# A decoder block on one core: attention's scores as float32r passes on padded q, values once per pair of heads, a bias copy, adaLN sums and the final norm moved

## The chip, the core and the metric

The kernel runs on one NeuronCore of a Trainium2 chip. It is one launch, and what counts is the device time of that launch in microseconds (us). The engines named below are PE (TensorE, matmuls), DVE (VectorE), ACT (ScalarE), POOL (GpSimd) and SP, whose queue issues most transfers. Each engine runs its instructions in order; a transfer is issued by the queue of an engine and then runs beside all of them. The profile is one execution recorded on the chip.

## What is computed

One block for 512 tokens of width 1024: a token mixer with 8 heads of block-sparse attention (64 wide) beside a pooling branch, then a mixture of 32 experts, then a last norm. With 512 tokens there are two blocks of 256 keys, and at most one fully past block can be selected, so the attention is causal attention with a relative bias.

```python
mod = (c_act @ w_ada[l] + b_ada[l])[:, None, :]
shift1, scale1, gate1, shift2, scale2, gate2 = jnp.split(mod, N_MOD, axis=-1)
h = rms_norm(x, norm1_g[l]) * (1 + scale1) + shift1
proj = h @ w_in[l]
q, k, v, u, z_gate = jnp.split(proj, split_pts, axis=-1)
y_attn = moba_attention(q, k, v, rel_bias) @ w_branch_attn[l]
y_pool = pool_mixer(u, pool_w[l], pool_scale[l]) @ w_branch_pool[l]
g_attn, g_pool = jnp.split(jax.nn.sigmoid(z_gate + b_gate[l]), N_BRANCHES, axis=-1)
mixed = (g_attn * y_attn + g_pool * y_pool) @ w_out[l]
x = x + gate1 * mixed
h2 = rms_norm(x, norm2_g[l]) * (1 + scale2) + shift2
x = x + gate2 * hier_moe(h2, ...)
...
return rms_norm(x, norm_f_g)
```

## The kernel before

All large products are float32. A projection is made of three float32r matmuls (`mm3`): each operand is split into a high part (ACT casts, L227) and a low part (DVE or POOL subtracts, L228), and high x high, high x low and low x high are summed in PSUM.

The program has these stages, in TensorE's order.

- Input stage, 0 to 71.6 us. x is normed and transposed, the first adaLN sums (ada_ps, L257) are made, and v, the fourth k and the first u are projected while their weights arrive. Six steps over the contraction (`first`) each bring a piece of w_ada and of w_in (wvk, L149) through SP. This stage is written out by hand: its engines run the instructions in the order of the program text. The low parts of the weights of k and u (kul) are made on POOL. The bias of the heads is made once as a row of 640 numbers per head (bias_sb); it goes to DRAM as bias_d (L376) and is then copied, 128 times per head, to bias_s in DRAM (L379, 8 x 128 x 640 numbers, 2.6 MB), from which each head reads its skewed 128 x 512 bias tile bt (L483, on SP). Both copies are issued by POOL's queue.
- Projections and attention, 71.6 to 250 us. q, k, u, the pooling branch's gates zp and its projection bp, in jobs of 12 or 24 matmuls. The attention of a pair of heads (hp = 0 to 3) runs between them. For each of four tiles i of 128 queries and each of the two heads e: scores s (L492) in fp32, on the 64 rows of that head, against the n = 128 (i + 1) keys so far; add bias and take the minimum (the q are negated) on DVE (L500); exp on ACT (L505); reciprocal and scaling on DVE (L507, L508); transposes tp in blocks of 128 (L511), copied to SBUF as pt by ACT or DVE (L514, L516); values y (L520), one fp32 matmul of 128 columns for each query tile i, key tile j and head e.
- Gates and branch projections of attention, 250 to 331 us: za and ba, eight column tiles cc each (`gated`). Beside the projections of 71.6 to 331 us run 32 steps `ada_step`: each loads 512 KB of w_ada (tile ada, two buffers, through SP) and adds it, scaled by a number of c, to gacc on DVE (L580), one in four over ACT and POOL (L577, L578). Sixteen steps make one row r of sums: gacc starts with a POOL memset (L568) and a load of b_ada (L569); at its end four small matmuls gs_ps (L586) sum it over the partitions, ACT copies the result (grow, L590), and a transfer writes it to rows_d, from where it is read back (L1020).
- Output projection, second norm, router (331 to 397 us); 16 pairs of experts (397 to 845 us), whose weights, 1 MB a load, come through SP into rings of buffers.
- Tail, 845 to 871 us: the last results are added in column ranges of 512, 256 and 256; ACT squares each token tile i in two halves (`square`, L1304), DVE forms the mean (L1307, L1329), POOL the power -0.5 (L1331), and `final` scales half a tile on ACT and half on DVE and issues the output's transfer, once for each of four token tiles.

Outside the input stage a scheduler orders the instructions of each engine, from the order of the program text, the dependences and the buffers of the pools.

## Time and profile before

| what | value |
|---|---|
| time, median of 3 runs | 874.46 us (870.32 to 875.41) |
| time of the profiled execution | 872.84 us |
| its span | 871.1 us (1.7 us lie around it) |
| PE busy | 831.2 us, 95% |
| DVE, ACT, POOL busy | 408.7, 238.9, 95.8 us |
| transfers | 265.36 MB, mean 305 GB/s |

The table is an average: in the experts' stage both TensorE and the transfers are full, in the first 331 us they are not full at the same time. So each stage is read for itself.

### The profile page before, as it was taken

Reading aid. Unit: us, or ns where it says so; the run is one execution under the profiler, and the core shown is the slowest. Engines: PE = TensorE matmul, PEld = TensorE weight load, DVE = VectorE, ACT = ScalarE, POOL = GpSimd, SP = SyncE. Lnnn points to the kernel's source line nnn. Section 1 sums busy time; section 2 is a strip of 40 time slices with the busy share of each in tenths; the row PEclk is TensorE's granted clock in tenths of the full one; section 3 lists DMA queues with packets and bytes.
Section 4 is the critical chain, followed back from the end, with each engine's and each line's share of the span. In section 5 each row is a group of like instructions: output and inputs, shape, how many; then the busy total and the mean of one; then the engine's idle time right before and its main releaser. Section 6 shows DMA issues by size and latency. Waiting matters only on the chain.

```text
span 871.1 us, 12304 instructions
## 1 busy us (share of the span) xinstructions
PE 831.2 (95%) x4890; PEld 496.4 (57%) x4890; DVE 408.7 (47%) x812; ACT 238.9 (27%) x478; POOL 95.8 (11%) x114
## 2 busy tenths in 40 slices
PE   6979999999999979999999999999999999999993
PEld 4758666676678747874445544554455445544542
DVE  4343546767537766672334333433343334333425
ACT  4222434443424324553111111111111111111204
POOL 5310003321103221141000000000000000000003
PEclk9999999999999989999999999999999999999997
DMA  9971324476357666958999999999999999999942
GB/s 294 345 290 41 103 90 122 145 243 202 94 187 246 198 258 231 374 225 350 370 420 419 420 420 419 420 419 420 420 420 420 420 419 420 420 420 419 405 137 100
DMA packets 72988, 265.36 MB, mean 305 GB/s; under 512 B 8280, under 2 KB 33708, under 8 KB 50398
## 3 DMA queue, kind: packets, MB, share of 16 engines
q1 hardware_dynamic: 71150, 261.18, 77.4%
q0 software_dynamic: 1600, 3.22, 1.0%
q8 instruction: 40, 0.66, 0.3%
q14 instruction: 22, 0.18, 0.1%
q10 hardware_dynamic: 176, 0.12, 0.0%
HBM read 262.37 MB, written 4.76 MB: 307 GB/s over the span
## 4 chain that ended last, share of the span: by engine, by line
PE 77%; DMA 10%; DVE 7%; issue 2%; ACT 1%; POOL 1%; SPq 1%; POOLq 0%; DVEq 0%; ACTq 0%
PE y_ps L1258 13%; PE g_ps L1233 13%; PE u_ps L1233 13%; PE c_ps L1271 7%; PE XT_ps L1006 6%; DMA ada<-in_w_ada_dram 5%; DVE gacc L580 3%; PE s L492 2%; DMA wvk<-in_w_in_dram 2%; PE o_ps L231 2%; PE o_ps L233 2%; PE o_ps L232 2%; DMA wq<-in_w_in_dram 1%; PE y L520 1%; PE tp L511 1%
## 5 line engine op out<-in xcount | busy, mean ns | idle before, releaser
L1233 PE MATMUL g_ps<-eg,XT 128*64 128x512 f32 x512 | 112.7, 592 | 0.1
L1233 PE MATMUL u_ps<-eu,XT 128*64 128x512 f32 x512 | 112.6, 592 | 0.0
L1258 PE MATMUL y_ps<-ed,HT 128*64 128x512 f32 x496 | 110.0, 595 | 0.0
L1242 DVE TENSOR_TENSOR H<-H,u_ps 128x512 f32<-128x512 f32 x16 | 11.0, 687 | 178.2 <-PE u_ps L1233 178.2
L1275 DVE TENSOR_TENSOR acc<-acc,c_ps 128x512 f32<-128x512 f32 (+1 forms) x132 | 78.5, 665 | 0.2 <-PE c_ps L1271 0.2
L1233 PEld LDWEIGHTS u_ps<-eu,XT 128*64 128x64 f32 x512 | 36.8, 137 | 73.1 <-issue 67.9
L1233 PEld LDWEIGHTS g_ps<-eg,XT 128*64 128x64 f32 x512 | 36.6, 137 | 73.0 <-issue 70.5
L1258 PEld LDWEIGHTS y_ps<-ed,HT 128*64 128x64 f32 x496 | 34.2, 137 | 63.6 <-issue 61.5
L1271 PE MATMUL c_ps<-Y,ohT 128*128 128x512 f32 (+1 forms) x264 | 67.9, 398 | 0.3 <-DVE Y L1353 0.2
L1006 PEld LDWEIGHTS <-h 128*128 128x128 f16 x1024 | 58.2, 113 | 6.0 <-issue 5.8
L1006 PE MATMUL XT_ps<-oh,h 128*128 128x128 f16 x1024 | 60.8, 219 | 0.7 <-DVE oh L984 0.6
L1271 PEld LDWEIGHTS c_ps<-Y,ohT 128*128 128x128 f32 x264 | 46.5, 189 | 21.7 <-issue 12.2
L580 DVE SCALAR_TENSOR_TENSOR gacc<-ada,cact,gacc 128x1024 f32<-128x1024 f32 x25 | 39.1, 1572 | 20.9 <-DMA ada<-in_w_ada_dram 20.2
L1000 ACT ACTIVATE XT<-XT_ps,col,a2col 128x128 f32<-128x128 f32 x64 | 29.2, 457 | 68.5 <-PE XT_ps L1006 53.1
L1265 DVE SCALAR_TENSOR_TENSOR y_ps<-y_ps,sw,g2row 128x512 f32<-128x512 f32 (+1 forms) x33 | 24.5, 743 | 49.7 <-PE y_ps L1258 49.7
L1250 ACT COPY HT<-HT_ps 128x512 f32<-128x512 f32 x16 | 9.4, 589 | 132.8 <-PE HT_ps L1248 132.8
L998 DVE TENSOR_SCALAR XT<-XT_ps,a2col,col 128x128 f32<-128x128 f32 x64 | 26.2, 410 | 41.5 <-ACT XT L1000 41.5
L1313 POOL MEMSET nf<- 1x128 f32 x1 | 0.2, 195 | 381.8 <-PE u_ps L1233 381.8
L227 ACT CAST Y<-y_ps 128x512 fp32r<-128x512 f32 x30 | 17.6, 585 | 86.5 <-DVE y_ps L1265 86.5
L1241 ACT ACTIVATE H<-g_ps 128x512 f32<-128x512 f32 x16 | 9.6, 597 | 82.0 <-PE g_ps L1233 82.0
L228 DVE TENSOR_TENSOR Y<-y_ps,Y 128x512 fp32r<-128x512 f32 x30 | 20.8, 692 | 21.1 <-ACT Y L227 21.1
L231 PE MATMUL za_ps<-hTh,za_h 128*128 128x512 f32 x64 | 25.0, 391 | 2.8 <-DVE ga L604 2.8
(291 smaller groups left out, 1374.9 us busy)
## 6 DMA issues: line engine op xcount, KB each, us to landing
eu<-in_w_expert_up_dram SPq DMA_DIRECT2D x60, 1024.0 KB, 15.8
ed<-in_w_expert_down_dram SPq DMA_DIRECT2D x60, 1024.0 KB, 19.6
eg<-in_w_expert_gate_dram SPq DMA_DIRECT2D x56, 1024.0 KB, 14.4
ada<-in_w_ada_dram SPq DMA_DIRECT2D x40, 512.0 KB, 4.7
eg<-in_w_expert_gate_dram SPq DMA_DIRECT2D x16, 512.0 KB, 8.2
ada<-in_w_ada_dram SPq DMA_DIRECT2D x4, 1024.0 KB, 9.2
zp<-in_w_in_dram SPq DMA_DIRECT2D x4, 1024.0 KB, 7.6
za<-in_w_in_dram SPq DMA_DIRECT2D x4, 1024.0 KB, 5.9
```

The costliest lines, as they stand in the source:

```text
L227: nc.scalar.copy(dst_h, src)
L228: sub.tensor_sub(dst_l, src, dst_h.bitcast(F32))
L231: nc.tensor.matmul(ps, lhsT=ah, rhs=bh, start=start, stop=False)
L580: nc.vector.scalar_tensor_tensor(g, t, cact[:, k : k + 1], g, op0=ALU.mult, op1=ALU.add)
L998: nc.vector.tensor_scalar(dst, src, a, b, op0=ALU.mult, op1=ALU.add)
L1000: nc.scalar.activation(dst, src, AF.Identity, bias=b, scale=a)
L1006: nc.tensor.matmul(ps[:, (k % 4) * P : (k % 4 + 1) * P], lhsT=ktile(h2[i][:, a], k), rhs=oh[:, i, :], start=(i == a == 0 and k == ks[0]), ...
L1233: mm = nc.tensor.matmul(ps[64 * e : 64 * e + 64, :], lhsT=XT[:, k, 64 * e : 64 * e + 64], rhs=ws[nm](k, e), start=(k == 0), stop=(k == KD ...
L1258: nc.tensor.matmul(ps[64 * e : 64 * e + 64, :], lhsT=HT[:, k, 64 * e : 64 * e + 64], rhs=rhs(k, e), start=(k == 0), stop=(k == KE - 1),)
L1265: nc.vector.scalar_tensor_tensor(ps, ps, sw, g2row[:, cs], op0=ALU.mult, op1=ALU.mult)
L1271: nc.tensor.matmul(ps, lhsT=ohT[:, i * P : (i + 1) * P], rhs=Y[:, a], start=(a == 0), stop=(a == 1))
L1275: nc.vector.tensor_add(accv(i)[:, cs], accv(i)[:, cs], ps)
```

## The change

Five things are changed.

1. The scores. q is kept in tiles qz, one slot per head of the pair, split into a high and a low part, 128 rows each, where the 64 rows of the other head are zero (POOL clears the two tiles once). k is split as well (kk). A score tile is then three float32r passes over 128 rows (`mm3`) in place of one fp32 matmul over 64.
2. The values. pt keeps the transposed weights of all query tiles of a head, ordered by key tile j, so that one matmul for key tile j serves all later queries: 512, 384, 256 and 128 columns. They stand after all four query tiles.
3. The order. The pairs of heads run in the order 3, 0, 1, 2, with other neighbours. The copies of the bias are written into the hand-ordered input stage.
4. The adaLN sums. Steps 16 to 19 are written into the second `pool_gated`, two instead of three steps follow each cc, and the second row's sums stand in the last cc.
5. The final norm. Squares in three column ranges, the mean of the first two for all tiles at once, the power for tiles 0 and 1 together and for 2 and 3.

```diff
+                    if n == 1:
+                        nc.gpsimd.dma_start(bias_d, bias_sb)
+                    if n + 2 == len(first):
+                        nc.gpsimd.dma_start(bias_s, bias_d.unsqueeze(1).broadcast_to([HEADS, P, 640]))
...
-    bias_d = dp.tile([HEADS, 640], F32, name="bias_d")
-    nc.gpsimd.dma_start(bias_d, bias_sb)
-
-    bias_s = dp.tile([HEADS, P, 640], F32, name="bias_s")
-    nc.gpsimd.dma_start(bias_s, bias_d.unsqueeze(1).broadcast_to([HEADS, P, 640]))
...
+    def k_tile(hp):
+        kk[hp] = at.tile([P, 2, 512], F32R, tag="kk", bufs=2, name=f"kk{hp}")
+        return kk[hp][:, 0], kk[hp][:, 1]
...
+    qz = [p.tile([P, 2, 2, 512], F32R, name=f"qz{n}") for n, p in enumerate((au, at))]
+    for z in qz:
+        for e in range(2):
+            nc.gpsimd.memset(z[64 - 64 * e : 128 - 64 * e, e].bitcast(F32), 0.0)
...
-    nc.vector.tensor_copy(kT[:, 3, :], ku_ps[0])
+    split(*k_tile(3), ku_ps[0])
...
-    for hp in range(4):
+    HPS = (3, 0, 1, 2)
+    for hp in HPS:
         job(f"q{hp}", raw["q"], hp * P, KD, hTh, hTl)
...
     def qk_proj(hp):
-        nc.scalar.mul(qT[:, hp, :], proj(f"q{hp}"), -(DH ** -0.5))
+        ps, z = proj(f"q{hp}"), q_of(hp)
+        for e in range(2):
+            rows = slice(64 * e, 64 * e + 64)
+            nc.scalar.mul(z[rows, e, 0], ps[rows], -(DH ** -0.5))
+            nc.vector.scalar_tensor_tensor(
+                z[rows, e, 1], ps[rows], -(DH ** -0.5), z[rows, e, 0].bitcast(F32), op0=ALU.mult, op1=ALU.subtract
+            )
         if hp < 3:
-            nc.vector.tensor_copy(kT[:, hp, :], proj(f"k{hp}"))
+            ps = proj(f"k{hp}")
+            split(*k_tile(hp), ps)
...
             for e in range(2):
-                nc.tensor.matmul(
-                    sps[e][:, 0:n], lhsT=qT[64 * e : 64 * e + 64, hp, i * P : (i + 1) * P],
-                    rhs=kT[64 * e : 64 * e + 64, hp, 0:n], start=True, stop=True,
-                )
-            pts = []
+                ts_ = slice(i * P, (i + 1) * P)
+                mm3(sps[e][:, 0:n], z[:, e, 0, ts_], z[:, e, 1, ts_], kh[:, 0:n], kl[:, 0:n], True, True)
...
-            for j in range(i + 1):
-                for e in range(2):
-                    nc.tensor.matmul(
-                        y_ps[64 * e : 64 * e + 64, i * P : (i + 1) * P],
-                        lhsT=vsb[:, j, (2 * hp + e) * DH : (2 * hp + e + 1) * DH],
-                        rhs=pts[e][:, j * P : (j + 1) * P], start=(j == 0), stop=(j == i),
-                    )
+        y_ps = ps1.tile([P, 512], F32, tag="y", name=f"y{hp}")
+        for j in range(NT):
+            for e in range(2):
+                nc.tensor.matmul(
+                    y_ps[64 * e : 64 * e + 64, j * P :],
+                    lhsT=vsb[:, j, (2 * hp + e) * DH : (2 * hp + e + 1) * DH],
+                    rhs=pts[e][:, 512 * j : 384 * j + 512], start=(j == 0), stop=(j == NT - 1),
+                )
         split(yAh[:, hp, :], yAl[:, hp, :], y_ps)
...
-        if n % 16 == 15:
-            ps = ps1.tile([P, 512], F32, tag="y", name=f"gs_ps{r}")
...
+        if n == 15:
+            ada_rows(0)
+
+    def ada_rows(r):
...
             gated("p", 4 * h + q, mpool[h][:, q, :], zp0 if h == q == 0 else None)
-            ada_step(8 * h + 2 * q)
-            ada_step(8 * h + 2 * q + 1)
-
+            for n in range(2 + h):
+                ada_step(8 * h + (2 + h) * q + n)
+
+    qk_proj(3)
+    pool_in(0)
+    attention(3)
     qk_proj(0)
-    pool_in(0)
+    pool_out(0)
+    qk_proj(1)
     attention(0)
-    qk_proj(1)
-    pool_out(0)
-    qk_proj(2)
-    qk_proj(3)
-    attention(1)
     pool_in(1)
...
         g = gated("a", cc, None)
+        if cc == 7:
+            ada_rows(1)
         (nc.vector if cc == 7 else nc.gpsimd).tensor_add(g, g, mpool[cc // 4][:, cc % 4, :])
...
-        for n in range(min(16 + 3 * cc, 32), min(19 + 3 * cc, 32)):
+        for n in range(min(20 + 2 * cc, 32), min(22 + 2 * cc, 32)):
             ada_step(n)
...
+    STEPS_F = (slice(0, 512), slice(512, 768), slice(768, 1024))
+
+    def square(i, n, junk):
+        cs = STEPS_F[n]
+        nc.scalar.activation(junk[:, 0 : cs.stop - cs.start], accv(i)[:, cs], AF.Square, accum_out=ssf[:, i, n : n + 1])
+
+    def mean0():
+
+        nc.vector.tensor_add(msf, ssf[:, :, 0], ssf[:, :, 1])
+        nc.vector.tensor_scalar(msf, msf, 1.0 / D, EPS, op0=ALU.mult, op1=ALU.add)
+
+    def rstd_f(*tiles):
+        ts = slice(tiles[0], tiles[-1] + 1)
+        nc.vector.scalar_tensor_tensor(msf[:, ts], ssf[:, ts, 2], 1.0 / D, msf[:, ts], op0=ALU.mult, op1=ALU.add)
+        nc.gpsimd.tensor_tensor(rsf[:, ts], msf[:, ts], neghalf.broadcast_to([P, len(tiles)]), op=ALU.pow)
...
     def final(i, p, nf):
-        ms = tiny("ms", [P, 1], F32, f"msf{p}_{i}")
-        nc.vector.scalar_tensor_tensor(ms, ssf[:, i, 1:2], 1.0 / D, msf[:, i : i + 1], op0=ALU.mult, op1=ALU.add)
-        r = tiny("rs", [P, 1], F32, f"rsf{p}_{i}")
-        nc.gpsimd.tensor_tensor(r, ms, neghalf, op=ALU.pow)
+        r = rsf[:, i : i + 1]
```

How the instructions come to stand shows at three places. First POOL in the input stage, before: kul is the low part of the weights of one step, and the copy of the bias stands between the splits of the third step and those of the fourth.

```order
L228 TENSOR_TENSOR wvl_371<-wvk_111,wvh_370 128x512
L228 TENSOR_TENSOR kul_375<-wvk_111,kuh_374 128x128 x2
L379 DMA bias_s<-bias_d 1024x1x640
L228 TENSOR_TENSOR wvl_428<-wvk_116,wvh_427 128x512
L228 TENSOR_TENSOR kul_432<-wvk_116,kuh_431 128x128 x2
L228 TENSOR_TENSOR kul_489<-wvk_122,kuh_488 128x2x128 x2
L228 TENSOR_TENSOR kul_569<-wvk_128,kuh_568 128x2x128 x2
```

POOL at the same place after the change.

```order
L228 TENSOR_TENSOR kul_377<-wvk_111,kuh_376 128x128 x2
L364 DMA bias_d<-bias_sb 8x640
L228 TENSOR_TENSOR wvl_431<-wvk_116,wvh_430 128x512
L228 TENSOR_TENSOR kul_435<-wvk_116,kuh_434 128x128 x2
L228 TENSOR_TENSOR kul_492<-wvk_122,kuh_491 128x2x128 x2
L228 TENSOR_TENSOR kul_572<-wvk_128,kuh_571 128x2x128 x2
L366 DMA bias_s<-bias_d 1024x1x640
L379 MEMSET ones 128x128
L422 MEMSET qz_705 64x1024 x2
```

The copy bias_s has moved behind the last kul, and the clearing of qz stands behind it.

Second, DVE at the first softmax step of the attention (L500: scores and the bias tile bt give sm and its minimum mn), before. q_l and k_l are low parts of weights of q and k.

```order
L228 TENSOR_TENSOR k_l<-wk_656,k_h 128x512
L476 COPY kT<-k_ps 128x512
L228 TENSOR_TENSOR q_l<-wq_650,q_h 128x512
L228 TENSOR_TENSOR q_l<-wq_652,q_h 128x512
L500 ISA sm_0_0_814,mn_0_0_815<-s_0_0_810,bt_0_805 128x128
L500 ISA mn_0_0_815 128x1
L500 ISA sm_0_1_826,mn_0_1_827<-s_0_1_811,bt_1_807 128x128
```

DVE at the same place after the change.

```order
L494 SCALAR_TENSOR_TENSOR qz_705<-q_ps,qz_705 64x512 x2
L228 TENSOR_TENSOR q_l<-wq_650,q_h 128x512
L228 TENSOR_TENSOR q_l<-wq_652,q_h 128x512
L522 ISA sm_0_0_796,mn_0_0_797<-s_0_0_788,bt_0_782 128x128
L522 ISA mn_0_0_797 128x1
L494 SCALAR_TENSOR_TENSOR qz_706<-q_ps,qz_706 64x512
L522 ISA sm_0_1_807,mn_0_1_808<-s_0_1_789,bt_1_784 128x128
L522 ISA mn_0_1_808 128x1
L529 RECIPROCAL rl_0_0_801<-l_0_0_799 128x1
L530 TENSOR_SCALAR sm_0_0_796<-sm_0_0_796,rl_0_0_801 128x128
L494 SCALAR_TENSOR_TENSOR qz_706<-q_ps,qz_706 64x512
```

The step that reads bt now stands ahead of the two low parts of the second q (qz_706), and less projection work lies before it: q of pairs 3 and 0, where q and k of pair 0, q of pair 1 and a part of its k lay.

Third, POOL between the two rows of adaLN sums, before. ga are the gated branch tiles, col is what is read back from rows_d.

```order
L578 TENSOR_TENSOR gacc_1631<-gacc_1631,ada_15_2183 128x1024
L1020 DMA col_2915<-rows_d_725 128x4 x2
L723 TENSOR_TENSOR ga_2223<-ga_2223,mpool_1610 128x512
L568 MEMSET gacc_2278 128x2048
L569 DMA gacc_2278<-in_b_ada_dram 1x16x128
L723 TENSOR_TENSOR ga_2290<-ga_2290,mpool_1610 128x512
```

POOL there after the change.

```order
L603 TENSOR_TENSOR gacc_1649<-gacc_1649,ada_15_2149 128x1024
L593 MEMSET gacc_2161 128x2048
L594 DMA gacc_2161<-in_b_ada_dram 1x16x128
L754 TENSOR_TENSOR ga_2255<-ga_2255,mpool_1628 128x512
L1051 DMA col_2931<-rows_d_731 128x4 x2
L754 TENSOR_TENSOR ga_2316<-ga_2316,mpool_1628 128x512
```

The memset and the load of the second row's gacc now stand ahead of the first ga and of the reads of rows_d.

## Rows read from the trace of the kernel before

**Rows 1.** Windows by stage: length, busy us (and instructions) by engine, PE clock, transfers.

```profile
core 0: us, PE busy (x) PEld busy (x) DVE busy (x) ACT busy (x) POOL busy (x), PEclk, DMA share, GB/s
0.00:71.60 71.60, 55.65 (x406) 41.75 (x407) 29.28 (x70) 24.70 (x52) 22.67 (x40) 0.98 0.90 295
71.60:250.00 178.40, 177.06 (x842) 123.74 (x840) 104.81 (x232) 68.98 (x154) 24.74 (x25) 1.00 0.38 124
250.00:331.00 81.00, 74.85 (x312) 56.42 (x312) 53.05 (x60) 26.36 (x49) 21.99 (x15) 0.96 0.68 235
```

**Rows 2.** Waits of PE: what for, us in total, times, longest.

```profile
PE v_ps L231 <- ACT hTh L227: 5.9, 3, 3.3
PE gs_ps L586 <- issue: 3.1, 1, 3.1
PE za_ps L231 <- DVE ga L604: 2.8, 1, 2.8
PE ada_ps L257 <- DMA ada<-in_w_ada_dram: 1.8, 1, 1.8
```

**Rows 3.** Windows, columns as in the first group: behind the wait at gs_ps.

```profile
322.20:330.00 7.80, 7.80 (x20) 3.28 (x21) 3.51 (x5) 1.51 (x3) 0.00 (x0) 0.60 0.57 228
```

**Rows 4.** Transfers, 20 to 62 us: queue, packets, MB, share of 16 engines.

```profile
q0 software_dynamic: 1072, 2.65, 16.1%
```

**Rows 5.** Chain of waits, 26 to 49 us: start, us, what.

```profile
26.46 14.50 DMA wvk<-in_w_in_dram
...
42.41 2.21 POOL kul L228 x2
44.62 3.34 SPq L149
...
48.65 12.99 DMA wq<-in_w_in_dram
```

**Rows 6.** Windows in the input stage.

```profile
42.00:48.00 6.00, 2.72 (x8) 1.89 (x7) 4.44 (x8) 1.87 (x5) 2.20 (x2) 0.77 0.53 211
```

**Rows 7.** Timeline of POOL, 40 to 72 us: start, us, instruction, idle time before it.

```profile
57.70 2.23 POOL L228 TENSOR_TENSOR kul<-wvk,kuh 128x256 fp32r<-128x256 f32 x2 [13.10 <-ACT kuh L227]
```

**Rows 8.** Transfers of tile bias_s: the copy is the longest, the others are bt.

```profile
DMA to landing us min/median/max: 2.6/4.6/22.4
```

**Rows 9.** Chain of waits, 88 to 96 us.

```profile
88.80 0.42 PE s L492 x4
89.22 0.43 PE k_ps L231
...
89.88 0.24 PE k_ps L233
...
93.98 0.63 PE s L492 x4
...
95.04 0.86 PE pw_ps L552 x2
```

**Rows 10.** Timeline of PE, 132 to 140 us.

```profile
132.81 0.91 PE L492 MATMUL s<-kT,qT 64*128 64x384 f32 x2
133.65 0.50 PE L231 MATMUL u_ps<-hTh,u_h 128*128 128x512 f32 x1
...
138.85 1.12 PE L492 MATMUL s<-kT,qT 64*128 64x512 f32 x2
139.90 0.50 PE L232 MATMUL u_ps<-hTl,u_h 128*128 128x512 f32 x1
```

**Rows 11.** PE's groups by shape, 71.6 to 331 us: busy us, mean ns, idle before.

```profile
L520 PE MATMUL y<-pt,vsb 128*64 128x128 f32 x160 | 16.9, 285 | 0.0
```

**Rows 12.** The page's groups: busy us, mean ns, idle time before and its cause.

```profile
L1265 DVE SCALAR_TENSOR_TENSOR y_ps<-y_ps,sw,g2row 128x512 f32<-128x512 f32 (+1 forms) x33 | 24.5, 743 | 49.7 <-PE y_ps L1258 49.7
```

**Rows 13.** Chain of waits, 261 to 267 us.

```profile
261.95 1.82 POOL gacc L568
...
264.06 2.46 DMA gacc<-in_b_ada_dram
```

**Rows 14.** Windows in the tail.

```profile
861.00:867.00 6.00, 0.00 (x0) 0.00 (x0) 2.11 (x5) 1.88 (x3) 1.09 (x2) 0.50 0.91 354
```

More of the change, by code (lines that the diff above doesn't have):

```diff
@@ L299, in step_ku @@
             mm3(ku_ps[n], kuh[:, m, n, :], kul[:, m, n, :], hTh[:, k, :], hTl[:, k, :], k == 0, k == KD - 1)
+    bias_d = dp.tile([HEADS, 640], F32, name="bias_d")
+    bias_s = dp.tile([HEADS, P, 640], F32, name="bias_s")
     with tc.manual_schedule(engines={getattr(mybir.EngineType, n) for n in ("PE", "Activation", "DVE", "Pool")}):
@@ L405, in block_kernel @@
     vsb = at.tile([P, NT, AW], F32, name="vsb")
-    qT = at.tile([P, 4, 512], F32, name="qT")
-    kT = at.tile([P, 4, 512], F32, name="kT")
+    kk = {}
+    def k_tile(hp):
+        kk[hp] = at.tile([P, 2, 512], F32R, tag="kk", bufs=2, name=f"kk{hp}")
+        return kk[hp][:, 0], kk[hp][:, 1]
     yPh = at.tile([P, 4, 512], F32R, name="yPh")
     yPl = at.tile([P, 4, 512], F32R, name="yPl")
-    ct1 = at.tile([P, C_W - C_KEEP], F32, name="ct1")
-    pw = at.tile([P, 4, P], F32, name="pw")
+    au, au_end = pool("au", side="right", bufs=1)
+    qz = [p.tile([P, 2, 2, 512], F32R, name=f"qz{n}") for n, p in enumerate((au, at))]
+    for z in qz:
+        for e in range(2):
+            nc.gpsimd.memset(z[64 - 64 * e : 128 - 64 * e, e].bitcast(F32), 0.0)
+    ct1 = au.tile([P, C_W - C_KEEP], F32, name="ct1")
+    pw = au.tile([P, 4, P], F32, name="pw")
     nc.sync.dma_start(ct1, consts[:, C_KEEP:])
@@ L416, in block_kernel @@
     nc.gpsimd.tensor_copy(ident16, ident)
-    au, au_end = pool("au", side="right", bufs=1)
     def utile(name):
@@ L486, in attention @@
             bts.append(bt)
-        y_ps = ps1.tile([P, 512], F32, tag="y", name=f"y{hp}")
+        z, (kh, kl) = q_of(hp), (kk[hp][:, 0], kk[hp][:, 1])
+        pts = [at.tile([P, 13 * P], F32, tag=f"pt{e}", name=f"pt{hp}_{e}") for e in range(2)]
         for i in range(NT):
@@ L580, in ada_step @@
             nc.vector.scalar_tensor_tensor(g, t, cact[:, k : k + 1], g, op0=ALU.mult, op1=ALU.add)
-        if n % 16 == 15:
-            ps = ps1.tile([P, 512], F32, tag="y", name=f"gs_ps{r}")
-            for v in range(2):
-                for h in range(2):
-                    j = 32 * (2 * v + h)
-                    nc.tensor.matmul(
-                        ps[j : j + 32, :], lhsT=onesf, rhs=gacc[r][:, v, 512 * h : 512 * h + 512], start=True, stop=True
-                    )
-            t = mo.tile([P, D], F32, tag="ad", bufs=2, name=f"grow{r}")[:, 0:512]
-            nc.scalar.copy(t, ps)
-            nc.scalar.dma_start(rows_d[r].rearrange("v (h n) -> (v h) n", h=2), t[0:P:32, :])
+        if n == 15:
+            ada_rows(0)
+    def ada_rows(r):
+        ps = ps1.tile([P, 512], F32, tag="y", name=f"gs_ps{r}")
+        for v in range(2):
+            for h in range(2):
+                j = 32 * (2 * v + h)
+                nc.tensor.matmul(
+                    ps[j : j + 32, :], lhsT=onesf, rhs=gacc[r][:, v, 512 * h : 512 * h + 512], start=True, stop=True
+                )
+        t = mo.tile([P, D], F32, tag="ad", bufs=2, name=f"grow{r}")[:, 0:512]
+        nc.scalar.copy(t, ps)
+        nc.scalar.dma_start(rows_d[r].rearrange("v (h n) -> (v h) n", h=2), t[0:P:32, :])
     def gate(which, cc):
@@ L625, in block_kernel @@
     pool_out(2)
-    attention(2)
+    qk_proj(2)
+    attention(1)
     zp0 = gate("p", 0)
@@ L632, in block_kernel @@
     pool_gated(0)
-    attention(3)
+    attention(2)
     pool_gated(1)
@@ L1289, in combine_half @@
             add(i, HALF[n], back(p, n, i, ohT, Y))
-    ssf = cp.tile([P, NT, 2], F32, name="ssf")
+    ssf = cp.tile([P, NT, 3], F32, name="ssf")
     msf = cp.tile([P, NT], F32, name="msf")
+    rsf = cp.tile([P, NT], F32, name="rsf")
     os_ = {}
@@ L1385, in last_pair @@
         for i in range(NT):
-            mean0(i)
+            square(i, 1, junk[i % 2])
         c2 = backs(2)
@@ L1389, in last_pair @@
             add(i, cols_[2], c2[i])
-            if i < 3:
-                square(i, 1, junk[i % 2])
+            square(i, 2, junk[i % 2])
+        mean0()
+        rstd_f(0, 1)
         final(0, p, nf)
-        square(3, 1, junk[1])
+        rstd_f(2, 3)
         for i in range(1, NT):
@@ L1493, in block_kernel @@
         for i in range(NT):
-            for h in range(2):
-                square(i, h, ex.tile([P, 512], F32, tag="HT", name=f"junkx{i}_{h}"))
-            mean0(i)
+            for n in range(3):
+                square(i, n, ex.tile([P, 512], F32, tag="HT", name=f"junkx{i}_{n}"))
             gain(i, "x", nf)
+        mean0()
+        rstd_f(0, 1, 2, 3)
+        for i in range(NT):
             final(i, "x", nf)
```

17 lines of the change are left out of this document (8 added, 9 removed).

## The prediction

> **What bounds the kernel now.** I read the windows by stage first, then the list of TensorE's waits, then the chain of waits in the places that these two point at. The first 331 us are the only part that the change touches, apart from the last 15 us. In it TensorE is busy 55.65 of 71.6 us, then 177.06 of 178.4, then 74.85 of 81 [rows 1]. So three different limits hold. In the first stage TensorE waits for data: 5.9 us of v_ps waits are among its losses [rows 2]. In the second (projections with attention between them) it is full, so only fewer or cheaper matmuls shorten it. In the third (gates, branch projections, adaLN sums) it waits 2.8 us at za_ps and 3.1 us at gs_ps [rows 2], and behind them it runs 7.8 us at a granted clock of 0.60, between its levels of 1.2 and 2.4 GHz [rows 3]; at the full level that work needs 0.60 x 7.8 = 4.7 us, so 3.1 more are lost there.
>
> **Bias copy (first stage).** The 2.6 MB copy bias_s goes out before the splits of step 3 and runs beside the loads of the stage. Its queue q0 took 16.1% of all engines' time from 20 to 62 us, that is 0.161 x 42 = 6.8 us [rows 4]. The chain shows who pays: a wvk load of 14.50 us, then kul on POOL for 2.21, then SP, which holds the next loads 3.34 us for that kul, then the wq load of 12.99 [rows 5]. From 42 to 48 us TensorE is busy 2.72 of 6 us, while the transfers fill only 0.53 of the engines [rows 6]: the half that works is not the half that the loads in front need. The change issues the copy after the last kul, so all of this goes. Bounds: at least the 3.34 us for which SP stood, since the wvk ahead of it comes that much sooner; at most the 5.9 us of waits, 1.8 on an ada load and 6 x (1 - 0.77) = 1.4 us of low clock [rows 2, 6], 9.1 in all. The loads themselves then come late next, so I take **-6 us** (-3.3 to -9.1). A rule bears on the 0.53: the Trainium skill, "DMA: Bandwidth & Descriptors", section "Rules for kernel authors", says that an outermost dimension under 16 keeps a DMA to at most that many engines; the copy's outermost is the 8 heads, hence half of 16, and the trace agrees. By that rule the copy is as slow after the move as before.
>
> What the move costs: the bt loads need the copy. In the trace the last kul ends at 57.70 + 2.23 = 59.9 us [rows 7]; 6 us earlier that is 54, the copy's landing 22.4 later is 76.3, and a bt load adds 2.6 to 4.6 [rows 8], so bt is there at 79 to 81. SP is in order and stands on that load, with wu behind it. DVE is in order too: its first softmax step waits for bt, with the q and k splits of the next heads behind it. TensorE leaves the first stage at 71.6 - 6 = 65.6, and by the order has 72 projection matmuls at 0.24 [rows 9] and some small score matmuls, 18 us in all, before the first transpose that needs that softmax: 83.6. From bt to that transpose lie one softmax step, an exp, a scaling and two splits of 0.74, about 3 us, so 82 to 84. I cost it at **0**, with the projections as cover, but the margin is 0 to 2 us; if it is gone every further us is paid in full.
>
> **Scores.** In fp32 a pair of heads costs 0.42 us at 128 columns and 0.63 at 256 [rows 9], where the two stand side by side; at 384 and 512 a head stands alone and takes 133.65 - 132.81 = 0.84 and 139.90 - 138.85 = 1.05 [rows 10]. A pair of heads: 0.42 + 0.63 + 2 x 0.84 + 2 x 1.05 = 4.83 us, four pairs 19.3. After, each head takes three float32r passes on 128 rows. The only such width in this stage is 512 at 0.24 [rows 9], narrower ones I scale: 3 x 0.24 x (1 + 3/4 + 1/2 + 1/4) = 1.8 us a head, four pairs 14.4. If 128 and 256 columns cost as much as 384, it is 3 x 0.24 x 3.25 = 2.34, 18.7. So -4.9 to -0.6, taken **-4**.
>
> Here a rule speaks against the change. The Trainium skill, "TensorEngine Tiling (Array Packing)", sections "Overview" and "Key Properties", gives two heads of 64 rows up to twice the speed as independent tiles, and says that a change of tiling mode drains the array. The trace shows the doubling at 128 and 256 only; were it had at 384 and 512 too, the scores before would cost 0.42 + 0.63 + 0.84 + 1.05 = 2.94 us a pair, 11.8 in all, and the change would lose 3 us. The order leaves a head alone there, so the row holds.
>
> **Values.** Before, 160 records of 128 columns are 16.9 us [rows 11]. After, each pair has four key tiles of 512 to 128 columns, both heads side by side. An fp32 matmul of 512 columns takes 0.86 (pw_ps) [rows 9], so 0.86 x 2.5 = 2.15 us a pair, or 3.0 where the first head's matmul goes out alone, as the order has it in each pair: 8.6 to 12. Part of the 16.9 is the end of a block that other work covers, so I take **-4.5** (-3 to -7).
>
> **Borders.** A float32r matmul right behind an fp32 block starts its successor after 0.43 us, not 0.24 [rows 9], 0.2 lost. Fewer such blocks stand in the order after: the scores are no longer fp32, and the values come in one or two blocks a pair, not four or five. By the order about 50 blocks become about 30: -4 us, between 0 (the passes on padded q may have a border of their own) and -6. I take **-3.5**.
>
> **New work on DVE and ACT.** Each q now takes two ACT scalings and two DVE steps of 64 rows in place of one ACT step; a DVE step of that kind takes 743 ns [rows 12]. 8 x 0.74 = 6 us on DVE. It is busy 104.81 of 178.4 us [rows 1], so about 111 of 166 after. It stays under TensorE, but in order, and the first half of the attention has the softmax, the splits and this together: I take **+2** (0 to +5). POOL's zeroing of qz lies behind the copy and far ahead of its readers: nothing. The stage: -4 - 4.5 - 3.5 + 2 = **-10** (-18 to +1).
>
> **adaLN sums (third stage).** In the chain the second row's gacc is zeroed on POOL (1.82) and loaded with b_ada (2.46) only after the first row's sums have gone out and come back [rows 13]. The change puts zeroing and load right behind the last POOL step of the first row, so 4.3 us leave the chain that ends in gs_ps1. The three losses above sum to 2.8 + 3.1 + 3.1 = 9.0. The 16 steps still run on two buffers of loads, and gs_ps1 now stands behind ba7, some us later in TensorE's order. So at least 2 and at most 9: **-5.5**.
>
> **Final norm.** Four pow steps become two, and the four finals no longer wait one for one. But from 861 to 867 us the output's transfers fill 0.91 of the engines [rows 14]: with the gaps gone 0.09 x 6 = 0.5 us is to be had. **-0.5** (-1.2 to +0.3, if the first final goes out later, behind the joint mean).
>
> **Sum:** -6 - 10 - 5.5 - 0.5 = -22, against the profiled execution's 872.84, gives 850.8. The median of the runs is 1.6 above that execution, so **852.5**. The expert stage follows: its loads wait on TensorE for their buffers, so a TensorE that comes 21 us sooner also starts them sooner.
>
> **Rivals.** (1) The copy binds. If it takes 27 us instead of 22.4, because wq and wk now share the engines with it at full rate, bt comes 5 us later, beyond the margin, DVE holds its queue and SP its wu: 3 to 5 us back, and half of the attention's gain with them: 852.5 + 4 + 5 = 861. For: the thin margin. Against: TensorE has 18 us of cover. Chance 0.17. (2) The scores don't become cheaper: narrow passes at their upper bound (-0.6), borders stay (0), DVE costs its 5: the stage gives -0.6 - 4.5 + 5 = 0, so 862.5. Chance 0.11. (3) The adaLN change does not do what it says: the loads pace the 16 steps, the 4.3 us turn into waiting for loads, and only the low clock's share is won, -2: 856, inside the range. It is part of the forecast's spread. (4) The loads of the experts bind. If that stream starts no earlier than now, what is won ahead of it is given back and only slack and tail remain, about -4: 870. Against: the loads wait for buffers. Chance 0.05. (5) Slower: DVE's order. With the qz steps and the wait for bt ahead of the softmax steps, TensorE would wait at each of the 16 groups of transposes and fall to its 1.2 GHz level between, as it did behind 6 us of waits in the third stage [rows 2, 3]. 16 x 1.5 = 24 us of waits, and 10 us of low clock: +34, 886. It decides from about 2 us of waiting in each group, and DVE at 0.67 of the stage does not suggest that. Chance 0.04.
>
> **How the numbers follow.** The forecast, 852.5, has 0.60, with its own range of 845 to 859; 0.03 goes to a larger gain than its bounds. The range for 8 in 10 reaches from 841 (all terms near their better bounds) to 866, which takes in the first two rivals and leaves out the last two and the far end of the first stage's gain. A measurement here tells about 1%, 8.7 us, from no change. Faster by more: 0.60 + 0.03 + 0.15 of rival 1 + 0.09 of rival 2 = 0.87; within 1%: the rest of these and rival 4, 0.08; slower: 0.05.
>
> **What would show it.** Right: v_ps waits nearly gone and the last ku matmul at 62 to 68 us; no transfer share of a half at 42 us; bt landing before the first softmax step needs it, or at most 2 us after; score passes of 512 columns at 0.24 and the stage from there to the first za_ps some 168 us long; gs_ps1 without a 3 us wait and clock 1.0 behind it; the expert stage unchanged in length. Wrong: a TensorE wait of several us at the first transposes, a wait of u_ps for its late loads, or narrow score passes of 0.2 us and more.

## The result, and the profile after

The changed kernel takes 859.74 us (median of 4 runs, 858.10 to 861.14) against 873.18 us of the kernel before beside it: a ratio of 0.985, with a 95% interval from 0.982 to 0.988, so 13.4 us faster. Its profiled execution is its fastest, with a span of 856.2 us against 871.1. The forecast was 852.5, in a range of 841 to 866.

Windows by stage of the changed kernel, cut at TensorE's marks (the end of the last ku matmul, the first za, the end of the last output-projection matmul); columns as in [rows 1]:

```profile
0.00:64.69 64.69, 55.70 (x406) 41.52 (x407) 30.57 (x70) 24.36 (x52) 26.90 (x44) 0.97 0.96 304
64.69:234.46 169.77, 165.48 (x778) 128.97 (x776) 106.94 (x240) 72.06 (x162) 24.80 (x25) 0.99 0.44 144
234.46:365.35 130.89, 125.26 (x554) 98.10 (x553) 87.98 (x128) 52.70 (x90) 32.83 (x27) 0.97 0.71 256
```

The same three marks in the kernel before:

```profile
0.00:71.63 71.63, 55.68 (x406) 41.75 (x407) 29.31 (x70) 24.73 (x52) 22.67 (x40) 0.98 0.90 294
71.63:249.79 178.16, 176.82 (x841) 123.74 (x840) 104.78 (x232) 68.95 (x154) 24.74 (x25) 1.00 0.38 125
249.79:380.36 130.57, 124.42 (x555) 97.05 (x554) 87.24 (x128) 52.69 (x90) 32.76 (x27) 0.97 0.74 263
```

The first stage is 6.9 us shorter, the second 8.4, the third together with the output projection not at all (130.57 and 130.89), and what follows is 490.7 us long in the one and 490.9 in the other. In the second stage TensorE's busy time fell by 11.3 us, from 176.82 to 165.48, but the stage by 8.4: 4.3 us are now waits.

These are single executions. A second profile of the changed kernel (of a run of 862.40 us, below) has 66.51, 173.13 and 130.47 us for the three, and in the nine profiles whose kernels have this first stage it ends between 62.88 and 66.51 us. A difference of 3 us in one stage of two profiles may be scatter.

Waits of TensorE in the changed kernel, first at v_ps, then all from 64 to 234 us, then all from 234 to 365:

```profile
PE v_ps L231 <- ACT hTh L227: 0.4, 1, 0.4
```

```profile
PE tp L533 <- DVE rl L529: 3.2, 1, 3.2
PE s L231 <- DVE mn L522: 1.0, 1, 1.0
```

```profile
PE za_ps L231 <- DVE ga L633: 2.7, 1, 2.7
PE o_ps L231 <- ACT wohl L865: 2.2, 1, 2.2
PE o_ps L232 <- DVE wol L866: 0.3, 1, 0.3
PE o_ps L232 <- DVE wohl L866: 0.3, 1, 0.3
```

The waits for v_ps of [rows 2] have shrunk to 0.4. The wait at gs_ps is gone, but one for the split weights of the output projection (wohl) has come in its place, and the wait at za_ps has stayed. The timelines of DVE and TensorE show what za_ps waits for:

```profile
293.74 2.27 DVE L605 SCALAR_TENSOR_TENSOR gacc<-ada,cact,gacc 128x1024 f32<-128x1024 f32 x1 [3.44 <-DMA ada<-in_w_ada_dram]
295.93 0.68 DVE L633 SCALAR_TENSOR_TENSOR ga<-ga,ba_ps 128x512 f32<-128x512 f32 x1
296.76 0.47 PE L231 MATMUL za_ps<-hTh,za_h 128*128 128x512 f32 x1 [2.71 <-DVE ga L633]
```

DVE stood 3.44 us for a load of w_ada, then did that adaLN step, and only then the ga that TensorE needed. From 296.7 to 300.9 us the granted clock was 0.60.

The bias copy, in the timeline of POOL: the last kul, and behind it the issue of the copy.

```profile
52.14 2.23 POOL L228 TENSOR_TENSOR kul<-wvk,kuh 128x256 fp32r<-128x256 f32 x2 [9.36 <-ACT kuh L227]
54.32 1.14 POOL L366 DMA_DIRECT2D bias_s<-bias_d  x1
```

The transfers of tile bias_s, and the window that [rows 6] shows of before:

```profile
DMA to landing us min/median/max: 2.7/5.1/16.0
```

```profile
42.00:48.00 6.00, 6.00 (x26) 4.52 (x25) 2.88 (x5) 1.24 (x2) 0.78 (x2) 1.00 1.04 388
```

TensorE is now full from 42 to 48 us, and so are the transfers. The copy lands at 54.3 + 16.0 = 70.3 us, 16.0 after its issue and not 22.4 [rows 8]. From 62 to 66 us nothing else is transferred, and the copy fills half of the engines' time:

```profile
q0 software_dynamic: 165, 0.84, 50.5%
```

The new scores and values, in the timeline of TensorE:

```profile
81.56 0.28 PE L231 MATMUL s<-kk,qz 128*128 128x256 f32 x1
81.67 0.28 PE L232 MATMUL s<-kk,qz 128*128 128x256 f32 x1
...
87.71 0.34 PE L231 MATMUL s<-kk,qz 128*128 128x384 f32 x1
87.89 0.34 PE L232 MATMUL s<-kk,qz 128*128 128x384 f32 x1
...
104.55 1.07 PE L545 MATMUL y<-pt,vsb 128*64 128x512 f32 x2
105.55 0.77 PE L533 MATMUL tp<-ct,sm 128*128 128x128 f32 x5
...
107.77 2.37 PE L545 MATMUL y<-pt,vsb 128*64 128x512 f32 x14
110.07 0.33 PE L533 MATMUL tp<-ct,sm 128*128 128x128 f32 x1
```

A pass of 256 columns starts its successor after 0.11 us and one of 384 after 0.18, where one of 512 takes 0.23: at these widths the passes scale with them. The values of one pair take 1.0 us for the first head's widest matmul, which goes out alone, and 2.3 for the rest.

The chain from the end of the third stage into the output projection:

```profile
306.97 0.82 PE gs_ps L615 x3
...
309.09 0.59 ACT grow L619
...
309.71 5.14 DMA rows_d<-grow
...
314.91 0.79 DVE wol L866
...
317.18 2.37 DVE wohl L866 x2
...
319.59 0.79 PE o_ps L232
```

And the window behind it:

```profile
317.60:322.00 4.40, 4.11 (x11) 2.79 (x12) 1.94 (x2) 0.00 (x0) 0.00 (x0) 0.61 1.03 401
```

The chain still runs through the second row of adaLN sums: its last sum, the copy grow, the transfer to rows_d, and only then these splits of the output projection's weights. The granted clock is down to 0.61 behind the wait here too.

### The profile page after: what moved, and what is told of

It is laid out like the page before. It is cut to its first block, busy times and chain, and to the rows that moved or that the text cites. A ratio compares the mean times of both kernels' runs of the same rounds, so it can differ in the third digit from the quotient of the medians.

```text
span 856.2 us, 12203 instructions
## 1 busy us (share of the span) xinstructions
PE 822.1 (96%) x4826; PEld 503.7 (59%) x4826; DVE 412.6 (48%) x816; ACT 242.2 (28%) x494; POOL 99.8 (12%) x116
## 4 chain that ended last, share of the span: by engine, by line
PE 82%; DMA 8%; DVE 5%; issue 2%; ACT 1%; POOL 1%; SPq 0%; DVEq 0%; POOLq 0%; ACTq 0%
PE y_ps L1289 13%; PE g_ps L1264 13%; PE u_ps L1264 13%; PE c_ps L1302 7%; PE XT_ps L1037 7%; DMA ada<-in_w_ada_dram 6%; DVE gacc L605 2%; PE o_ps L232 2%; PE o_ps L233 2%; PE o_ps L231 1%; PE y L545 1%; DMA xt<-in_x_dram 1%; PE v_ps L231 1%; PE za_ps L231 1%; PE v_ps L233 1%
## 5 line engine op out<-in xcount | busy, mean ns | idle before, releaser
L1302 PEld LDWEIGHTS c_ps<-Y,ohT 128*128 128x128 f32 x264 | 46.5, 189 | 21.8 <-issue 12.2
## 6 DMA issues: line engine op xcount, KB each, us to landing
eu<-in_w_expert_up_dram SPq DMA_DIRECT2D x60, 1024.0 KB, 16.4
```

Of the source, the lines that this page charges most:

```text
L1302: nc.tensor.matmul(ps, lhsT=ohT[:, i * P : (i + 1) * P], rhs=Y[:, a], start=(a == 0), stop=(a == 1))
```

## The experiments

From the two traces I formed a theory, called the stream theory below: the second adaLN row takes 70 us from its first load to its last step (253.7 to 323.3 us before, 237.7 to 307.9 after), paced by two buffers; its first load has to wait until the first row's sums have left gacc, and these wait, through the one PSUM buffer that they share with the values y, for the last pair's values. The memset and the b_ada load, which the change moved, would then not be on the path. (Part of this did not hold, as the runs below show: with other PSUM buffers the first load went out 1.9 us ahead of the sums, with values per tile 5.1 us.) Each expectation below says which rival stood against it. Times are medians; the kernel before took 870.4 to 872.3 us beside them, and ratios are against it.

**Bias copy alone**, in the kernel before:

```diff
+                    if n == 1:
+                        nc.gpsimd.dma_start(bias_d, bias_sb)
+                    if n + 2 == len(first):
+                        nc.gpsimd.dma_start(bias_s, bias_d.unsqueeze(1).broadcast_to([HEADS, P, 640]))
...
-    nc.gpsimd.dma_start(bias_d, bias_sb)
...
-    nc.gpsimd.dma_start(bias_s, bias_d.unsqueeze(1).broadcast_to([HEADS, P, 640]))
```

> The kernel before, with nothing but the two copies of the bias written into the input stage as after the change. Theory: the copy stands in front of the loads of the first stage, and its move alone ends that stage 7 us earlier (71.6 to 64.7); all of this reaches the end, so 866 us against 873. Rival: the later copy makes the first softmax steps wait for bt, as here q and k of pair 0 and q of pair 1 come first with no more cover than that; then 2 to 5 us of the 7 come back as a wait at the first transposes and the end is 868 to 871.

Measured: 862.59 us, ratio 0.990 (0.987 to 0.993). The first stage ends at 65.92 us, the second is as long as before, and the third with the output projection is shorter, though its code is that of the kernel before:

```profile
0.00:65.92 65.92, 56.11 (x406) 42.31 (x407) 29.35 (x70) 24.46 (x52) 22.74 (x40) 0.97 0.94 303
65.92:244.26 178.34, 176.82 (x841) 123.76 (x840) 104.48 (x232) 68.95 (x154) 24.73 (x25) 1.00 0.39 131
244.26:369.39 125.13, 121.27 (x555) 96.34 (x554) 86.87 (x128) 52.71 (x90) 32.78 (x27) 1.00 0.76 275
```

So this one small edit has most of the whole gain. The end is lower than the 866 expected, and the rival, a wait for bt, did not come. In this profile 5.7 us are won in the first stage and 5.4 in the third with the output projection. The last row says that this stage is not worth a fixed time: the same instructions took 130.6 us at a clock of 0.97 and 125.1 at 1.00.

**Bias copy back**, in the changed kernel, the reverse:

> The changed kernel with the copies of the bias issued where they were before the change. Theory: the copy's place alone is worth 7 us in the first stage, and this stage is in front of everything: 865 to 868, with that stage ending at 70 to 72 us. Rival: in the changed kernel something else, the waits of the second and third stages, takes most of that back: under 4 us slower, below 863.

Measured: 868.22 us, ratio 0.997 (0.995 to 0.999), in 10 runs, a little above the 865 to 868 of the theory; the first stage ends at 72.45 us. All the rest of the change together is worth some 2 us (1 to 4 by the interval). The waits at v_ps and the hole from 42 to 48 us are back:

```profile
PE v_ps L231 <- ACT hTh L227: 5.8, 3, 3.4
42.00:48.00 6.00, 3.13 (x15) 2.28 (x14) 2.70 (x5) 1.75 (x4) 2.20 (x2) 1.00 0.73 284
```

**adaLN steps back**, in the changed kernel:

```diff
-            for n in range(2 + h):
-                ada_step(8 * h + (2 + h) * q + n)
+            ada_step(8 * h + 2 * q)
+            ada_step(8 * h + 2 * q + 1)
...
-        if n == 15:
-            ada_rows(0)
+        if n % 16 == 15:
+            ada_rows(r)
...
-        if cc == 7:
-            ada_rows(1)
...
-        for n in range(min(20 + 2 * cc, 32), min(22 + 2 * cc, 32)):
+        for n in range(min(16 + 3 * cc, 32), min(19 + 3 * cc, 32)):
```

> The changed kernel with the adaLN steps as before the change (two steps in the second pool_gated, three behind each cc, the second row's sums in the last step). The prediction's term: the 4.3 us of memset and b_ada load return to the chain, so 3 to 6 us slower than the changed kernel, 863 to 866. Theory formed from the two traces (stream): the second row takes 70 us from its first load to its last step in both kernels, paced by two buffers, and the first load waits for the first row's sums; how the steps are written hardly matters, so 859 to 861, within 1.5 us of the changed kernel.

Measured: 854.25 us, ratio 0.980 (0.977 to 0.983). Neither side expected this: without its adaLN part the change is 4.2 to 5.5 us better (against 858.42 and 859.74). The intervals just touch (0.982 to 0.988 for the changed kernel); the single runs lie from 853.15 to 857.53, those of the changed kernel from 857.53 to 862.40. In its waits from 234 to 365 us the one at gs_ps has returned and those at the output projection are gone:

```profile
PE gs_ps L615 <- issue: 3.2, 1, 3.2
PE za_ps L231 <- DVE ga L633: 2.7, 1, 2.7
```

Its profile is of its slowest run (857.5) and has 130.02 us for third stage and output projection, as the changed kernel has, so that it doesn't show where the other three runs gain their 3 us. The second row's first load goes out at 237.3 us in it, as in the changed kernel (237.7).

**Sums in other PSUM buffers**, in the changed kernel:

```diff
-        ps = ps1.tile([P, 512], F32, tag="y", name=f"gs_ps{r}")
+        ps = ps1.tile([P, 512], F32, tag="sc", bufs=2, name=f"gs_ps{r}")
```

> The changed kernel; the adaLN sums gs_ps take their PSUM tile from the scores' two buffers and no longer from the single buffer of the values y, so the first row's sums need not wait until the last pair's values are out. Stream theory: the second row starts 10 to 20 us earlier, its last step and the start of the output projection without waits come with it, TensorE is then full from 235 us on: 5 to 9 us faster than the changed kernel, 851 to 855. Rival (weights): the splits of the output projection's weights on ACT and DVE set its start whatever the adaLN row does: at most 2 us faster, 858 to 860.

Measured: 852.08 us, ratio 0.979 (0.976 to 0.982). The second row's first load goes out at 220.3 us and not at 237.7, its last step ends at 288.6 and not at 307.9; the row still takes 68 us. The third stage and the output projection:

```profile
235.27:358.75 123.48, 120.69 (x546) 97.15 (x545) 80.92 (x125) 52.32 (x89) 30.84 (x23) 0.99 0.73 261
```

The time is the stream theory's, not the rival's. But the theory also wanted the waits at the start of the output projection to go, and these stayed, as the rival said; what is gone is the wait at za_ps:

```profile
PE o_ps L231 <- ACT wohl L865: 2.1, 1, 2.1
PE o_ps L231 <- ACT grow L619: 0.7, 1, 0.7
```

**Without the second row's steps**, in the changed kernel:

```diff
+        if n >= 16:
+            return
         t = mo.tile([P, D], F32, tag="ad", bufs=2, name=f"ada2_{n}")
```

> The changed kernel without the 16 steps of the second adaLN row (gate and shift of the second half come from b_ada alone; 8.4 MB of loads, 12 DVE and 4 ACT and POOL steps are left out). Stream theory: this row is what the third stage waits for, so its waits and the low clock behind them go and 8 to 11 us are won against the changed kernel: 849 to 852. Rival (weights): the splits of the output projection still come too late, only the wait at za_ps goes: 3 to 4 us, 855 to 857.

Measured: 850.13 us, ratio 0.977 (0.974 to 0.980). 124.37 us for the same piece: the row that is not there frees as much as the row that starts early. Here too the wait at za_ps is gone, and the one for wohl is as long as ever, with no step of the row in front of it:

```profile
PE o_ps L231 <- ACT wohl L867: 2.1, 1, 2.1
```

**The changed kernel again**, beside the next three:

> The changed kernel once more, unaltered, so that the others of this group stand beside it on the same chip. Its earlier time was 859.7 us, against 873.2 for the kernel before: if the two agree, 858 to 861; if its third stage is sensitive to the moment at which TensorE's clock falls, it may lie anywhere from 855 to 862.

Measured: 858.42 us (857.53 to 862.40), ratio 0.984 (0.981 to 0.988).

**Scores in fp32**, in the changed kernel:

```diff
-                mm3(sps[e][:, 0:n], z[:, e, 0, ts_], z[:, e, 1, ts_], kh[:, 0:n], kl[:, 0:n], True, True)
+                hr = slice(64 * e, 64 * e + 64)
+                nc.tensor.matmul(
+                    sps[e][:, 0:n], lhsT=z[hr, 0, 0, ts_].bitcast(F32), rhs=kh[hr, 0:n].bitcast(F32), start=True, stop=True
+                )
```

> The changed kernel with its scores again in fp32 on 64 rows (q and k kept whole, without padding, split and clearing). Stream theory: the scores cost TensorE 20.0 us in place of 16.4 and the second stage is 3 to 5 us longer, but the second adaLN row starts behind that stage, so all of it reaches the end: 3 to 5 us slower than the changed kernel on the same chip. Rival: DVE's and ACT's extra steps for the split give as much back as the passes win: within 1 us of it.

Measured: 858.81 us, ratio 0.985 (0.981 to 0.989), 0.4 us over the changed kernel beside it: the rival. Its second stage:

```profile
64.33:234.03 169.70, 168.41 (x745) 119.11 (x744) 98.75 (x232) 68.20 (x154) 24.25 (x25) 1.00 0.42 139
```

TensorE is busy 168.41 us there, 2.9 more than with the new scores, and waits 1.3, 3.0 less (1.8 more and 5.2 less against the second profile of the changed kernel). DVE is busy 98.75, 8.2 less.

**Values per tile**, in the changed kernel:

```diff
+            for j in range(i + 1):
+                for e in range(2):
+                    o = 384 * j + 128 * i
+                    nc.tensor.matmul(
+                        y_ps[64 * e : 64 * e + 64, i * P : (i + 1) * P],
+                        lhsT=vsb[:, j, (2 * hp + e) * DH : (2 * hp + e + 1) * DH],
+                        rhs=pts[e][:, o : o + P], start=(j == 0), stop=(j == i),
+                    )
```

> The changed kernel with the values again in matmuls of 128 columns for each query tile, key tile and head. The prediction's term was 4.5 us; the traces show TensorE's spacing for the values as 15.1 us before and 13.2 after. Theory: the merged values win little, 1 to 3 us, since the first of a pair goes out alone: 1 to 3 us slower than the changed kernel. Rival: merging holds all values of a pair back to its end, and the first adaLN row's sums wait for the single PSUM buffer of the values; per tile they are out sooner and the kernel is no slower or up to 2 us faster.

Measured: 860.10 us, ratio 0.986 (0.982 to 0.991), 1.7 us over the changed kernel beside it: in the theory's 1 to 3, but within what the runs scatter. The two sides of it are both there: the second stage is 176.67 us long, 3.5 to 7 more than in the two profiles of the changed kernel, and the third with the output projection 127.72, some 3 less.

```profile
63.34:240.01 176.67, 172.62 (x881) 133.28 (x880) 109.02 (x242) 72.75 (x162) 24.24 (x25) 0.99 0.44 145
240.01:367.73 127.72, 123.38 (x549) 98.33 (x546) 84.02 (x127) 52.89 (x90) 33.16 (x27) 0.97 0.72 254
```

**Other PSUM buffers and adaLN steps back together** (the edits of both):

> The changed kernel with two edits: gs_ps in the scores' PSUM buffers, and the adaLN steps written as before the change. Stream theory: with the early start of the second row its steps end long before TensorE needs them, whichever way they are written: 851 to 853, as with the first edit alone. Rival: the old way of writing them was worth 5 us by itself (854.3 against 859.7) for a reason of its own, as it leaves the second pool_gated with fewer steps on DVE; then it adds to the other edit: 846 to 849.

Measured: 853.43 us (849.88 to 856.12), ratio 0.980 (0.976 to 0.984). The two edits do not add. But the row does not start early here, as the theory wanted: its first load goes out at 237.0 us, hardly ahead of the changed kernel's 237.7. Still the wait at za_ps is gone, and the third stage with the output projection is the shortest but one of all profiles, with the wait at gs_ps back in it:

```profile
234.62:357.44 122.82, 119.95 (x549) 96.45 (x546) 86.26 (x127) 52.93 (x90) 33.03 (x27) 1.00 0.74 270
PE gs_ps L615 <- issue: 2.9, 1, 2.9
```

**Without both rows' steps**, in the changed kernel:

```diff
+        if n == 15:
+            ada_rows(0)
+        return
         t = mo.tile([P, D], F32, tag="ad", bufs=2, name=f"ada2_{n}")
```

> The changed kernel without the 32 steps of both adaLN rows (16.8 MB of loads and their DVE, ACT and POOL steps are left out; both rows come from b_ada alone). Theory formed from the runs so far: in the second stage the matmuls saved by the new scores come back as waits, because DVE, in order, stands up to 17 us on loads of w_ada in front of the softmax steps. Then without both rows that stage is 164 to 167 us long in place of 170 to 173, with no wait at tp or s over 1 us, and the end is 2 to 5 us below the 850.1 of the kernel without the second row: 845 to 848. Rival: the waits come from DVE's own longer list (the splits of q and k), and remain: 849 to 851.

Measured: 842.97 us, ratio 0.969 (0.965 to 0.972), 2 us under the theory's 845 to 848. The second stage has no wait of TensorE left:

```profile
62.97:226.33 163.36, 163.36 (x777) 128.30 (x776) 88.05 (x228) 68.11 (x158) 15.23 (x21) 1.00 0.32 102
```

This also takes 12 DVE steps, 18.9 us, off DVE's list in that stage, so it tells that the adaLN steps cause the waits, not whether their length or their waiting does. The timelines of DVE and TensorE in the changed kernel show both at the wait of 3.2 us, which ends at 198.98:

```profile
196.78 1.86 DVE L605 SCALAR_TENSOR_TENSOR gacc<-ada,cact,gacc 128x1024 f32<-128x1024 f32 x1 [1.07 <-DMA ada<-in_w_ada_dram]
198.56 0.27 DVE L530 TENSOR_SCALAR sm<-sm,rl 128x128 f32<-128x128 f32 x1
198.98 0.45 PE L533 MATMUL tp<-ct,sm 128*128 128x128 f32 x1 [3.23 <-DVE rl L529]
```

DVE waits 1.07 us for a load and takes 1.86 for the step; then come the scalings of sm that the transposes need.

**Bias copy and other PSUM buffers**, in the kernel before:

> The kernel before with two edits: the copies of the bias moved as in the change, and gs_ps in the scores' PSUM buffers. Stream theory: the second adaLN row starts earlier and the third stage loses its waits, 2 to 5 us below the 862.6 with the bias alone: 857 to 860. Rival (the third stage's losses in that kernel were only a matter of the clock, and it ran there in 125 us already): no change, 861 to 863.

Measured: 863.69 us, ratio 0.992 (0.990 to 0.995): the rival, 1.1 us over the same kernel without the second edit, which is within the scatter. There the first row's sums move by 1.3 us only, from 0.3 us behind the first za to 1.0 ahead of it, so the buffer of y was not what held them.

**Half tiles of w_ada**, in the changed kernel with the other PSUM buffers:

```diff
+        for h in range(2):
+            t = mo.tile([P, 512], F32, tag="ad", bufs=4, name=f"ada2_{n}_{h}")
+            c0 = (2 * r + 2 + v) * D + 512 * h
+            nc.sync.dma_start(t, wad[k * P : (k + 1) * P, c0 : c0 + 512])
+            g = gacc[r][:, v, 512 * h : 512 * h + 512]
```

> The changed kernel with gs_ps in the scores' PSUM buffers (852.1) and the steps of w_ada in halves of 512 columns on four buffers, the same SBUF. If two buffers and the time of a 512 KB load set the pace, four loads of 256 KB in flight shorten it: DVE's waits for loads fall by a third, the waits at tp and s in the second stage go, 1 to 4 us: 848 to 851. Rival: twice as many DVE steps and issues, with DVE in order, cost what the shorter loads win: 852 to 855.

Measured: 851.11 us, ratio 0.977 (0.975 to 0.979). Between the two sides: 1 us under the same kernel with whole tiles, which these runs can't tell from nothing, and TensorE still waits 4.8 us at s in the second stage. The second row takes 68 us here too (222.5 to 290.4), so the two buffers of 512 KB are not shown to set its length. Four complete versions beat both kernels: 854.25, 852.08, 853.43 and 851.11, the second by one changed line.

## Why the prediction came out as it did

The sign and the range held; the sum was 22 us where 13.4 were measured, and the time is 7.2 us above the forecast. That it still lies in the range is in part luck. The bias copy alone is worth 8 to 10 us, more than its 6; all the other terms, 16 us together, gave 2.2 (bias copy back) to 3.7 (13.4 less the 9.8 of the bias copy alone). The terms, one by one:

- **Bias copy, -6 (-3.3 to -9.1).** Right in mechanism: SP's longest hold for a kul is 2.5 us where it was 7.4, the longest wvk load 12.2 where it was 19.0, the waits at v_ps are nearly gone, and in the profile the stage is 6.9 us shorter. Alone it gave 9.8 us by the medians and 8.7 by the ratio, of which 5.7 lie in the first stage of its profile; its removal cost 8 to 10 by the medians. The rest lies in the third stage, which ran faster behind it. Why that stage's waits and clock fare better there is not settled.
- **bt's cover, 0.** It held. The copy landed at 70.3 us, earlier than the 76.3 worked out, because it took 16.0 us and not 22.4: it shared the engines with fewer loads. The first bt loads, issued at 70.3 us (bt loads take 2.7 to 7.0), did not hold the first softmax step (77.1), and TensorE did not wait at the first transposes (82.4). The Trainium skill's rule on an outermost dimension under 16 ("DMA: Bandwidth & Descriptors", "Rules for kernel authors") agrees with the copy's 50.5% of the engines when it runs alone; what the prediction drew from it, that the copy is as slow after the move as before, was wrong by 6.4 us.
- **Scores, -4, with +2 for DVE.** By TensorE's spacing they cost 20.0 us before and 16.4 after, so the passes are as cheap as taken. The step that failed is the +2. With fp32 scores the kernel is as fast (858.81 against 858.42), and its profile says why: TensorE's busy time in the stage is 2.9 us less with the new scores, its waits 3.0 more. DVE's added steps, behind its in-order waits for w_ada, turn TensorE's saving into waits; without the adaLN steps, or without the added ones, these are gone or short. The times alone could not tell the 2 us that were forecast from none. The Trainium skill's rule that speaks against the padding ("TensorEngine Tiling (Array Packing)", "Overview") did not decide here: TensorE's time for the scores did fall.
- **Values, -4.5, and borders, -3.5.** The first is mis-sized: by TensorE's spacing the values took 15.1 us before and 13.2 after, -1.9, since a pair takes 1.0 + 2.3 = 3.3 us and not 2.15 to 3.0. Of the 11.3 us less of TensorE's busy time 5.8 are then left for the borders and the rest; no run takes these, or the new order of the pairs, back alone. With values per tile the second stage is 3.5 to 7 us longer. But the merged values free the PSUM buffer of y late: the first row's sums stand 2.1 us behind the first za, with values per tile 1.0 ahead of it, and the second row's first load 3.2 behind, there 6.1 ahead. There the wait at za_ps is gone and the third stage with the output projection some 3 us shorter; 1.7 us remain at the end, within the scatter.
- **adaLN sums, -5.5 (-2 to -9).** The second step that failed: the third stage with the output projection is as long as before, and taking this whole part back makes the kernel 4.2 to 5.5 us faster. Three things were wrong. First, the 4.3 us of memset and b_ada load [rows 13] were not on DVE's path in the kernel before; its first step of the second row waited 0.53 us for that load:

```profile
266.61 2.48 DVE L580 SCALAR_TENSOR_TENSOR gacc<-ada,cact,gacc 128x1024 f32<-128x1024 f32 x2 [0.53 <-DMA gacc<-in_b_ada_dram]
```

Second, the wait at gs_ps was exchanged, not won. In the profile the third stage ends 4.9 us earlier relative to its start, and the output projection gives 5.2 us back, waiting for wohl at a clock of 0.61. Every profile with the sums in the last cc has that wait of 2.1 to 2.2 us, also without any step of the row, and every one with the sums behind the last step has some 3 us at gs_ps in its place.

Third, the wait at za_ps stayed, as DVE still stood on loads of w_ada. Where that wait is 2.4 to 2.8 us long (six profiles, the kernel before and the changed one among them), the third stage with the output projection takes 130.0 to 132.0 us; where it is 0.8 or less (the other eight), 122.7 to 127.7. Without the second row it is gone, so the row's steps cause it.

What else takes it away is not settled. In the changed kernel other PSUM buffers do: the sums come 14 us and the row's first load 17 us earlier, so there they did hang on y, and this gives 6 to 8 us. But with the old steps in addition it is gone as well, although the row starts at 237.0, and in the two kernels that are the one before with the bias copy moved it is 0.8 or less. Why the old way of writing the steps is faster than the new one, where the row starts no earlier, stays open. Rival 3, the loads pace the steps, fits the time that DVE stands on them (12.2 us in 6 waits from 225 us on); what sets the row's 66 to 75 us is not shown.
- **Final norm, -0.5.** From the start of the last matmul to the end of the span it is 13.9 us before (857.2 to 871.1) and 13.4 after (842.8 to 856.2); the two other profiles with the old norm have 13.9, the ten others with the new one 12.8 to 13.8. The transfers fill the engines in it, as said:

```profile
847.00:852.40 5.40, 0.00 (x0) 0.00 (x0) 1.41 (x2) 1.33 (x2) 0.37 (x1) 0.51 0.99 381
```

- **Rivals.** The first (copy binds), the fourth (expert loads bind: what comes after the output projection is as long as before) and the fifth (TensorE at half clock through attention) did not happen. Of the second, the part on DVE did, not the one on the passes' cost; of the third, that the 4.3 us were not to be had.

## What to carry to other kernels

A bulk copy that nobody needs soon costs most where it is issued in front of loads that somebody waits for; move the issue, and look who reads it first. A saving on the busiest engine is only worth what the in-order engine beside it can follow with: undo the edit alone to see it. Before a step is taken out of a chain, look how long the engine behind it stood waiting for it: here 0.53 us, where the step had 4.3. When a chain hangs on a stream of loads, look for what lets its first transfer start; in the changed kernel that was one shared PSUM buffer, in the kernel before it was not.

## What was not expected of the hardware

The same instructions of third stage and output projection took 130.6 us in one kernel and 125.1 in another that differs only in the first stage, 3.1 of them in TensorE's busy time at a granted clock of 0.97 against 1.00. Both have a wait of 3.1 us at gs_ps. Behind it the clock is 0.60 for 7.8 us in the kernel before [rows 3], and does not fall at all with the bias copy alone:

```profile
314.10:322.00 7.90, 7.90 (x33) 4.89 (x34) 6.59 (x10) 3.79 (x6) 1.41 (x5) 1.00 0.89 329
```

So the length of one wait did not tell here whether the clock falls, and a fall costs 3 us of such a stage. Two variants have to be compared over several runs: the changed kernel's own medians were 859.7 and 858.4, and its single runs lay between 857.5 and 862.4.
